# The last projection of a decoder trunk: operand sums and the residual by accumulating DMA in place of GpSimd additions

## Chip, cores and metric

The kernel runs on one NeuronCore of a Trainium2 chip. The metric is the device time of one execution in microseconds (us); the kernel before took 1645.27 us (median of three runs, 1644.04 to 1647.09). Engines are named as in the profile: PE (TensorE, the matmuls), PEld (its weight loads), DVE (VectorE), ACT (ScalarE), POOL (GpSimd), SP (SyncE, which here only issues DMAs). L686 is line 686 of the kernel.

## What is computed

A trunk of two residual layers and a final norm on x of 1024 tokens by 1024 channels, all in float32:

```python
h_res = x
h_res = h_res + even_layer(rmsnorm(h_res, norm_g[0]))    # state-space and pooling mixers
h = rmsnorm(h_res, norm_g[1])
z = h @ w_in                                             # 1024 x 8192
x_in, b_gate, c_gate, g = split(z, 4)
conv = causal_conv3(c_gate * x_in) + conv_b
y = b_gate * conv * silu(g)                              # 1024 tokens x 2048 channels
h_res = h_res + y @ w_out                                # w_out 2048 x 1024: the last projection
return rmsnorm(h_res, final_g)
```

The change concerns the last two lines: `y @ w_out`, the residual added to it, and the way into the final norm.

## The kernel before

**Precision.** Every large matmul runs on float32 values split in two parts, a rounded part h and the rest l = x - h (`split_to`, L78: ScalarE writes h, VectorE writes l, L81/L82 or with a scale L84/L85). A product is three matmuls: h weight by h activation, h by l, l by h.

**The last projection** is one product of 2 x 2 blocks by Winograd's form of Strassen's scheme: seven products of half-size operands instead of eight, each with operands that are blocks or sums of blocks. The contraction's halves are channels 0 to 1023 and 1024 to 2047 of y; the other halves are the first and second 512 tokens (`H0`, `H1`) and the even and odd 128-row blocks of the output. The seven products are numbered and run in the order `JT = (1, 5, 7, 6, 4, 2, 3)`. Each takes four weight tiles of 128 x 1024 (p = 0 to 3), so there are 28 weight tiles w = 0 to 27, product `JT[w // 4]`, tile p = w % 4.

**Steps.** A step t (`j_mm`, L1004) is the 24 matmuls of one weight tile: eight blocks n, three matmuls each. Steps 0 to 23 work on 512 columns; the last product (3) runs in two quarters of 256 columns, so steps 24 to 31 are half steps with tiles 24 to 27 twice. Results land in six halves of three PSUM tiles in turn. `j_post(t - 1)` (L1020), run at the beginning of step t, adds step t - 1's result into one to three quarters of the two output tiles `o` of row pair p (product 1 is copied by ScalarE instead).

**What each product needs.** Activations live in one tile `x` of eight blocks: x0(n) is the H0 half and x1(n) the H1 half of block n; b22 is a separate tile in the slots `td0` and `td1`. In place, block by block, `jb_sum` (L937) makes the operands of products 5, 7, 6 and 4 ("T4"), and `jb_split` splits them; products 1, 2 and 3 take plain blocks. On the weight side a tile S per p is kept in place: `jw_load` (L957) loads blocks on SP's queue, `jw_sum` (L973) makes the sums of products 5, 7, 6 and 3 on GpSimd (16 in all), `jw_split` (L983) splits into a ring of two h and two l tiles. GpSimd also does half of the block sums of products 5, 7 and 6, all eight of T4's, and the residual: `res_load` brings a 128 x 1024 block of the residual stream on SP's queue, `res_add` (L1040) adds it to `o` on GpSimd, eight times.

**What sets the order.** It is written out by hand. Every engine executes its own list in order and waits for semaphores; SP's and POOL's queues are also in order. `j_pre[t]` (from L1321) lists what is put on the engines ahead of step t's matmuls: splits one step before use, weight sums two, weight loads three. `sc_tail` (L1313) does the same for the last seven steps of the layer's input projection (`run_pairs`, L728), where loads and first splits of the last projection begin. `end2()` (L1504) returns the last two products of the layer before (`b * t`, VectorE, and a store of each to `y2d`), which are run ahead of step 0's matmuls. From step 18 on squares of finished rows are summed for the final norm, and from step 28 on VectorE and GpSimd scale the output by the norm and SP stores it.

Of the kernel before, what the change touches and what calls it, by code (L numbers as in the profile page):

```python
# [8 lines left out]
F32 = mybir.dt.float32  # L9
F32R = mybir.dt.float32r  # L10
I32 = mybir.dt.int32
AF = mybir.ActivationFunctionType
ALU = mybir.AluOpType

P = 128
T = 1024
# [11 lines left out]
def trunk(ctx: ExitStack, tc: tile.TileContext, a: dict, out: bass.AP):  # L28
# [4 lines left out]
    wp = ctx.enter_context(tc.tile_pool(name="wp", bufs=2))  # L33
# [5 lines left out]
    V, A, G, PE, S = nc.vector, nc.scalar, nc.gpsimd, nc.tensor, nc.sync  # L39
    LD = nc.scalar  # L40
    ctr = [0]

    def slot(tag, shape, dtype=F32):
        ctr[0] += 1
        return sp.tile(shape, dtype, tag=tag, name=f"{tag}_{ctr[0]}")
# [27 lines left out]
    def act_tiles(k, shape=(T,)):  # L73
        t = act_slot(k, [P, 2, *shape])
        act[k] = (t[:, 0], t[:, 1])
        return act[k]

    def split_to(h, l, src, scale=None, e=None):  # L78

        if scale is None:  # L80
            A.activation(h, src, AF.Copy)  # L81
            (e or V).tensor_tensor(out=l, in0=src, in1=h, op=ALU.subtract)  # L82
        else:
            A.activation(h, src, AF.Copy, scale=scale)  # L84
            V.scalar_tensor_tensor(out=l, in0=src, scalar=scale, in1=h, op0=ALU.mult, op1=ALU.subtract)  # L85
# [51 lines left out]
    def at(d, s, f):  # L137
        d.setdefault(s, []).append(f)
# [42 lines left out]
    y2d = dp.tile([16, P, T], F32, name="y2d")  # L181
    hrd = [dp.tile([P, T], F32, name=f"hrd{k}") for k in range(NK)]
# [45 lines left out]
    def tt(e, o, x, y, op):  # L228
        e.tensor_tensor(out=o, in0=x, in1=y, op=op)  # L229
# [169 lines left out]
    def u_load(k, tag):  # L399
        t = slot(tag, [P, 8, NC])  # L400
        LD.dma_start(t, ud[k].rearrange("(g h) j c -> (h j) g c", g=8))
        s5["U"][k] = t
# [205 lines left out]
    H0, H1 = slice(0, 512), slice(512, T)  # L608
# [298 lines left out]
    J_ = {"T": {}, "o": {}, "w": {}, "raw": {}, "h": {}, "bank": {}, "ring": 0, "acc": [None] * 3}  # L907
    JT = (1, 5, 7, 6, 4, 2, 3)
    JO = {0: (HB[0], HB[1]), 1: (HB[4], HB[5]), 2: (HB[2], HB[3]), 3: (HB[6], HB[7])}

    def y2_load(o, n0, n, hs):
        S.dma_start(o, y2d[n0 : n0 + n, :, hs].rearrange("n p t -> p n t"))

    def x_load(k, hs):

        if "x" not in J_:
            J_["x"] = slot("big", [P, 8, T])
        y2_load(J_["x"][:, 2 * k : 2 * k + 2, hs], 2 * k, 2, hs)

    def b21_load(k):  # L920
        y2_load(J_["x"][:, 2 * k : 2 * k + 2, H1], 8 + 2 * k, 2, H0)

    def y22_load(k):
        if k % 2 == 0:
            J_["y22", k // 2] = slot(f"td{k // 2}", [P, 4, 512])
        y2_load(J_["y22", k // 2][:, 2 * (k % 2) : 2 * (k % 2) + 2], 8 + 2 * k, 2, H1)

    def x0(n):
        return J_["x"][:, n, H0]

    def x1(n):
        return J_["x"][:, n, H1]

    def b22(n):
        return J_["y22", n // 4][:, n % 4]

    def jb_sum(i, n, e):  # L937
        if i == 5:
            tt(e, x0(n), x1(n), x0(n), ALU.subtract)
        elif i == 7:  # L940
            tt(e, x1(n), b22(n), x1(n), ALU.subtract)
        elif i == 6:
            tt(e, x0(n), b22(n), x0(n), ALU.subtract)
        elif i == 4:
            tt(e, x0(n), x1(n), x0(n), ALU.subtract)

    def jb_split(i, n):
        if n % 2 == 0:
            J_["B", i, n // 2] = act_tiles(4 * (JT.index(i) % 2) + n // 2, (2, 512))
        h, l = J_["B", i, n // 2]  # L950
        src = {1: x0, 5: x0, 7: x1, 6: x0, 4: x0, 2: x1, 3: b22}[i](n)
        split_to(h[:, n % 2], l[:, n % 2], src, 0.5)


    JS = ("t9", "t6", "t4", "t5")

    def jw_load(w):  # L957
        i, p = JT[w // 4], w % 4
        src = {1: (2 * p,), 5: (2 * p + 1, 9 + 2 * p), 7: (2 * p + 1,), 6: (9 + 2 * p,), 4: (9 + 2 * p,),
               2: (8 + 2 * p,), 3: (8 + 2 * p,)}[i]  # L960
        r = J_["raw", w] = []
        for j, m in enumerate(src):
            ctr[0] += 1
            if i == 1:
                t = J_["S", p] = slot(JS[p], [P, T])
            elif i == 5 and p % 2:
                t = slot(f"t{j}", [P, T])
            else:
                t = wp.tile([P, T], F32, tag="raw", name=f"raw_{ctr[0]}")
            S.dma_start(t, scout[m])  # L970
            r.append(t)

    def jw_sum(w):  # L973
        i, p = JT[w // 4], w % 4
        r = J_["raw", w]
        if i == 5:
            tt(G, r[0], r[0], r[1], ALU.add)
        elif i == 7:
            tt(G, J_["S", p], J_["S", p], r[0], ALU.subtract)
        elif i in (6, 3):  # L980
            tt(G, J_["S", p], r[0], J_["S", p], ALU.subtract)

    def jw_split(w):  # L983
        i, p = JT[w // 4], w % 4
        if i == 3 and p > 1:
            t = slot(f"td{p - 2}", [P, 2, T], F32R)
            h, l = t[:, 0], t[:, 1]
        else:
            ctr[0] += 1
            h = wp.tile([P, T], F32R, tag="whi", name=f"whi_{ctr[0]}")  # L990
            l = wp.tile([P, T], F32R, tag="wlo", name=f"wlo_{ctr[0]}")
        J_["w", w] = (h, l)
        split_to(h, l, J_["S", p] if i in (1, 7, 6, 3) else J_["raw", w][0])

    def j_slot(t):

# [36 lines left out]
            for d, x in {5: ((1, 0),), 7: ((3, 1), (2, 0)), 6: ((1, 1), (2, 2), (3, 3)), 4: ((2, 2),), 2: ((0, 0),)}[i]:  # L1033
                tt(V, q[d], q[x], bk, ALU.add)

    def res_load(m):
        J_["h", m] = slot(f"t{2 + m // 2 % 2}", [P, T])
        S.dma_start(J_["h", m], hrd[m])

    def res_add(m):  # L1040
        o = J_["o", m // 2][m % 2]
        tt(G, o, o, J_["h", m], ALU.add)

    def j_sq2(p):

        o = J_["o", p][1]
        if p == 0:
            J_["ss"] = slot("t1", [P, T])
            A.activation(J_["ss"], o, AF.Square)
        else:  # L1050
            J_["sq"] = slot("t0", [P, T])
            A.activation(J_["sq"], o, AF.Square)
            tt(V, J_["ss"], J_["ss"], J_["sq"], ALU.add)
        A.activation(o, o, AF.Copy, scale=gf[:, 2 * p + 1 : 2 * p + 2])
# [33 lines left out]
    win, wout, glu, scin, scout, pw = a["win"], a["wout"], a["glu"], a["scin"], a["scout"], a["pw"]  # L1088
# [46 lines left out]
    for k in range(8):  # L1135

        s = 6 + k // 2
        t, x = t_work(k), x_work(k - 1) if k else [lambda: None] * 2
        b = [lambda k=k: z_build(k + 2)] if k < 6 else []
        n = [lambda k=k: u_load(k + 1, UT[(k + 1) % 2])] if k < 7 else []  # L1140
        if k % 2 == 0:
            o = [lambda k=k, i=i: odd_work[k // 2 - 1][i]() for i in range(4)] if k else [lambda: None] * 4
# [160 lines left out]
    for k in range(4):  # L1303
# [7 lines left out]


    sc_tail = {-2: [lambda: jw_load(0), lambda: jw_load(1)],  # L1313
               1: [lambda: jw_load(4)],
               2: [lambda: jw_load(2), lambda: [x_load(k, H0) for k in range(4)]],
               3: [lambda: jw_load(3), lambda: [x_load(k, H1) for k in range(4)]],
               4: [lambda: [jb_split(1, n) for n in range(4)]],
               5: [lambda: jw_split(0), lambda: [jb_split(1, n) for n in range(4, 8)], lambda: jw_load(5)]}


    j_pre, j_mid = {}, {}  # L1321
    NS = 32
    for w in range(4, 28):
        at(j_pre, w - 2, lambda w=w: jw_sum(w))
    for w in range(1, 28):
        at(j_pre, w - 1, lambda w=w: jw_split(w))
    for w in range(6, 28):
        at(j_pre, w - 3, lambda w=w: jw_load(w))
    for x in range(6):
        i = JT[x + 1]  # L1330
        for n in range(8):
            if x == 0:
                at(j_pre, n // 2, lambda i=i, n=n: jb_sum(i, n, G if n % 2 else V))
            at(j_pre, 4 * x + n // 2, lambda i=i, n=n: jb_split(i, n))
    for x in range(1, 6):
        for n in range(8):
            at(j_pre, 4 * x + n // 2 - 1, lambda i=JT[x + 1], n=n: jb_sum(i, n, G if i == 4 or n % 2 else V))
    for k in range(4):
        at(j_pre, 1 + k // 2, lambda k=k: y22_load(k))
        at(j_pre, 5 + k, lambda k=k: b21_load(k))  # L1340
    for p in range(4):
        at(j_pre, 12 + p, lambda p=p: res_load(2 * p + 1))
        at(j_pre, 14 + p, lambda p=p: res_add(2 * p + 1))
        at(j_pre, 17 + p, lambda p=p: res_load(2 * p))
        at(j_pre, 19 + p, lambda p=p: res_add(2 * p))
        at(j_pre, 18 + p, lambda p=p: j_sq2(p))
        at(j_pre, 22 + p, lambda p=p: j_sq(p, H0))
    rH, rQ = j_rms(H0, False), [j_rms(at_q(q), True) for q in range(2)]
# [150 lines left out]
    late = []  # L1499
    for t in range(NS):  # L1500
        if t:
            j_post(t - 1)
        else:
            late = end2()  # L1504
        for f in j_pre.get(t, []):
            f()
        for f in late:
            f()
        late = []
        j_mm(t, j_mid.get(t, {}))  # L1510
    j_post(NS - 1)
    for f in j_pre[NS] + rQ[1]:
# [71 lines left out]
```

## Time and profile before

| what | value |
|---|---|
| median of three runs (lowest, highest) | 1645.27 us (1644.04, 1647.09) |
| the profiled execution: its own time | 1644.73 us |
| its span | 1642.9 us |
| mean granted PE clock | 0.977 |
| PE, DVE, ACT, POOL busy | 96%, 71%, 34%, 47% of the span |

The span is the time from the first to the last instruction; the execution's own time is 1.8 us longer, and lies 0.54 us under the median. Times in the trace count from the span's start. "Busy" of PE counts overlapping matmuls by their modelled ends, so a busy PE can still run slower than it could. An idle time is put down to the engine whose semaphore came last.

### The profile page before, as it was taken

How to read it: one execution, taken by the hardware profiler on the slowest of the kernel's cores; microseconds unless marked ns; L12 is line 12 of the kernel's file. 1: busy time of each engine (PE TensorE's matmuls, PEld its weight loads, DVE VectorE, ACT ScalarE, POOL GpSimd, SP SyncE). 2: the span in 40 equal slices, each digit the busy share in tenths (PEclk: the TensorE clock that was granted, in tenths of full speed). 3: DMA queues.
4: the chain of work that ended last, by engine and by line, in shares of the span. 5: the costliest groups of instructions: out<-in, count | busy, mean ns of one | idle time of the engine just before them, and what ended most of it. 6: DMA issues, size and time to landing. Idle time of an engine off the chain costs nothing.

```text
span 1642.9 us, 19135 instructions
## 1 busy us (share of the span) xinstructions
PE 1573.6 (96%) x7138; PEld 1301.5 (79%) x7138; DVE 1164.3 (71%) x1308; ACT 559.4 (34%) x840; POOL 772.2 (47%) x686
## 2 busy tenths in 40 slices
PE   9899999999999999999879999999999999997996
PEld 7688888877788788888658888888888888875776
DVE  5545655688555776652798696868677786899986
ACT  5245111123353433332433233332323232432363
POOL 6952599707322532101465353434353443458643
PEclk9999999999999999999879999999999999999997
DMA  6232632214687432233211212212121212454242
GB/s 212 94 124 90 159 110 84 77 63 137 187 285 240 145 115 78 77 116 136 95 37 67 78 52 77 78 52 102 53 77 52 77 52 92 165 204 151 81 153 104
DMA packets 94348, 181.83 MB, mean 111 GB/s; under 512 B 16432, under 2 KB 53040, under 8 KB 93744
## 3 DMA queue, kind: packets, MB, share of 16 engines
q1 hardware_dynamic: 55584, 93.05, 16.9%
q10 hardware_dynamic: 38672, 87.57, 16.3%
q8 instruction: 57, 0.93, 0.2%
q14 instruction: 35, 0.29, 0.1%
HBM read 141.85 MB, written 42.93 MB: 112 GB/s over the span
## 4 chain that ended last, share of the span: by engine, by line
PE 54%; DVE 10%; issue 1%; DMA 1%; ACT 1%; POOL 1%; DVEq 0%; ACTq 0%
PE acc L686 44%; PE acc L1018 5%; PE acc L114 4%; DVE a L85 3%; DVE wlo L82 2%; PE acc L837 1%; DVE t L229 1%; DVE big L229 1%; DVE ws L82 1%; DMA t<-in_glu 0%; DVE a L82 0%; POOL t L229 0%; DVE B L229 0%; DMA hpd<-t 0%; PE aux L168 0%
## 5 line engine op out<-in xcount | busy, mean ns | idle before, releaser
L686 PE MATMUL acc<-a,ws 128*128 128x512 f32 x1920 | 451.4, 391 | 3.9 <-DVE LR L229 1.6
L686 PEld LDWEIGHTS acc<-a,ws 128*128 128x128 f32 x1920 | 361.7, 189 | 81.5 <-ACT a L81 3.1
L114 PE MATMUL acc<-a,whi 128*128 128x512 f32 x1440 | 395.0, 396 | 2.6 <-DVE t L229 2.6
L114 PEld LDWEIGHTS acc<-a,whi 128*128 128x128 f32 x1440 | 269.8, 190 | 58.1 <-issue 4.0
L229 POOL TENSOR_TENSOR t<-t,t 128x512 f32<-128x512 f32 (+2 forms) x85 | 158.7, 1867 | 302.8 <-DVE ws L82 183.7
L81 ACT ACTIVATE ws<-t 128x512 fp32r<-128x512 f32 x200 | 125.8, 630 | 338.7 <-PE acc L686 199.8
L686 PE MATMUL acc<-big,ws 128*128 128x512 f32 x960 | 230.8, 396 | 10.8 <-DVE big L82 3.9
L686 PEld LDWEIGHTS acc<-big,ws 128*128 128x128 f32 x960 | 182.8, 191 | 52.3 <-DVE ws L82 5.5
L114 PE MATMUL acc<-a,wlo 128*128 128x512 f32 x720 | 222.8, 391 | 0.0
L82 DVE TENSOR_TENSOR ws<-t,ws 128x512 fp32r<-128x512 f32 x200 | 182.6, 913 | 32.5 <-ACT ws L81 30.7
L82 DVE TENSOR_TENSOR wlo<-raw,whi 128x1024 fp32r<-128x1024 f32 (+2 forms) x67 | 92.6, 1386 | 100.1 <-ACT whi L81 100.0
L114 PEld LDWEIGHTS acc<-a,wlo 128*128 128x128 f32 x720 | 136.0, 189 | 29.0
L1018 PE MATMUL acc<-a,whi 128*128 128x512 f32 (+1 forms) x448 | 137.3, 390 | 3.2 <-ACT whi L81 1.6
L229 DVE TENSOR_TENSOR t<-t,acc 128x512 f32<-128x512 f32 x140 | 94.9, 680 | 51.0 <-PE acc L686 50.9
L686 PE MATMUL acc<-td,ws 128*128 128x512 f32 x480 | 118.2, 395 | 0.3 <-DVE td L82 0.3
L81 ACT ACTIVATE whi<-raw 128x1024 fp32r<-128x1024 f32 (+2 forms) x67 | 63.5, 952 | 143.7 <-PE acc L114 120.8
L229 POOL TENSOR_TENSOR t<-C,LR 128x1024 f32<-128x1024 f32 (+1 forms) x18 | 41.7, 2320 | 143.2 <-PE aux L491 64.9
L686 PEld LDWEIGHTS acc<-td,ws 128*128 128x128 f32 x480 | 91.2, 190 | 21.3 <-issue 1.4
L1018 PE MATMUL acc<-a,wlo 128*128 128x512 f32 (+1 forms) x224 | 88.7, 396 | 16.6 <-DVE wlo L82 16.6
L1018 PEld LDWEIGHTS acc<-a,whi 128*128 128x128 f32 x448 | 86.6, 199 | 20.5 <-DVE a L85 2.4
L229 POOL TENSOR_TENSOR raw<-raw,raw 128x512 f32<-128x512 f32 (+1 forms) x22 | 32.0, 1455 | 128.3 <-DVE ws L82 121.0
L81 ACT ACTIVATE ws<-raw 128x512 fp32r<-128x512 f32 x80 | 50.0, 626 | 74.4 <-PE acc L686 51.7
(283 smaller groups left out, 2138.2 us busy)
## 6 DMA issues: line engine op xcount, KB each, us to landing
raw<-in_scin ACTq DMA_DIRECT2D x32, 512.0 KB, 4.0
t<-in_scin ACTq DMA_DIRECT2D x32, 512.0 KB, 4.3
raw<-in_win ACTq DMA_DIRECT2D x29, 512.0 KB, 3.6
raw<-in_scout SPq DMA_DIRECT2D x24, 512.0 KB, 4.1
t<-ud ACTq DMA_DIRECT2D x16, 512.0 KB, 4.3
raw<-in_wout ACTq DMA_DIRECT2D x16, 512.0 KB, 3.7
big<-y2d SPq DMA_DIRECT2D x12, 512.0 KB, 5.6
ud<-t SPq DMA_DIRECT2D x8, 512.0 KB, 2.9
```

The source lines that it names most:

```text
L81: A.activation(h, src, AF.Copy)
L82: (e or V).tensor_tensor(out=l, in0=src, in1=h, op=ALU.subtract)
L85: V.scalar_tensor_tensor(out=l, in0=src, scalar=scale, in1=h, op0=ALU.mult, op1=ALU.subtract)
L114: PE.matmul(acc[:, n * 512 : n * 512 + 512], lhsT=w, rhs=x[:, n * 512 : n * 512 + 512], start=first and i == 0, stop=last and i == 2)
L229: e.tensor_tensor(out=o, in0=x, in1=y, op=op)
L686: PE.matmul(bank, lhsT=wt, rhs=x[:, k], start=k == 0 and j == 0, stop=k == 3 and j == 2)
L837: PE.matmul(u.acc[:, hs], lhsT=w, rhs=x[:, hs], start=k == 0 and j == 0, stop=k == NK - 1 and j == 2)
L1018: PE.matmul(bank, lhsT=w, rhs=x[:, n % 2, c], start=n == 0 and j == 0, stop=n == 7 and j == 2)
```

## The change

All of it is in the last projection.

- Weight sums: the tile of the first block is completed in place by a DMA that adds the second block from DRAM (`accum_op=add`, issued on GpSimd's queue), without GpSimd adding. Where a difference is wanted (products 7 and 3) ScalarE first negates the tile in place. 16 accumulating transfers and 8 negations take the place of 16 loads and 16 GpSimd sums. The sign of product 7's weights turns, and that of its activations with it.
- T4: ScalarE negates x0 (two blocks at a time) and a DMA adds B21 from `y2d`: four negations, four accumulating transfers.
- Residual: `res_load` goes; `res_add` is an accumulating transfer from DRAM straight into `o`.
- All block sums of products 5, 7 and 6 run on VectorE.
- Product 3 reads B22 from `x` again (four new loads, `b22_load`), so `td0` and `td1` are free earlier and the splits of tiles 26 and 27 move to steps 18 and 20.
- Times: sums of product 5 in steps 0 and 1 (the first in the layer before), of 7 in steps 3 to 6, of 6 in 8 to 11, T4 in 9 to 12, of 3 in 13 to 16, residual in 14 to 17 and 18 to 21. Loads of B21 move from steps 5 to 8 to steps 12 to 15.
- The last two products of the layer before run in steps 1 and 2 instead of together in step 0.

The core of the diff:

```diff
         elif i == 7:
-            tt(e, x1(n), b22(n), x1(n), ALU.subtract)
+            tt(e, x1(n), x1(n), b22(n), ALU.subtract)
         elif i == 6:
             tt(e, x0(n), b22(n), x0(n), ALU.subtract)
-        elif i == 4:
-            tt(e, x0(n), x1(n), x0(n), ALU.subtract)
+    def neg(t):
+        A.activation(t, t, AF.Copy, scale=-1.0)
+    def plus(t, src):
+        G.dma_start(t, src, accum_op=ALU.add)
+    def t4_sum(k):
+        x = J_["x"][:, 2 * k : 2 * k + 2, H0]
+        neg(x)
+        plus(x, y2d[8 + 2 * k : 10 + 2 * k, :, H0].rearrange("n p t -> p n t"))
+    def b22_load(k):
+        y2_load(J_["x"][:, 2 * k : 2 * k + 2, H0], 8 + 2 * k, 2, H1)
...
     def jw_load(w):
...
+        if i == 1:
+            t = J_["S", p] = slot(JS[p], [P, T])
+        elif i == 5 and p > 1:
+            t = slot(f"t{p - 2}", [P, T])
+        else:
+            t = wp.tile([P, T], F32, tag="raw", name=f"raw_{ctr[0]}")
+        J_["raw", w] = t
+        S.dma_start(t, scout[{1: 2 * p, 5: 2 * p + 1, 4: 9 + 2 * p, 2: 8 + 2 * p}[i]])
     def jw_sum(w):
         i, p = JT[w // 4], w % 4
-        r = J_["raw", w]
-        if i == 5:
-            tt(G, r[0], r[0], r[1], ALU.add)
-        elif i == 7:
-            tt(G, J_["S", p], J_["S", p], r[0], ALU.subtract)
-        elif i in (6, 3):
-            tt(G, J_["S", p], r[0], J_["S", p], ALU.subtract)
+        t = J_["raw", w] if i == 5 else J_["S", p]
+        if i in (7, 3):
+            neg(t)
+        plus(t, scout[{5: 9 + 2 * p, 7: 2 * p + 1, 6: 9 + 2 * p, 3: 8 + 2 * p}[i]])
...
     def res_add(m):
-        o = J_["o", m // 2][m % 2]
-        tt(G, o, o, J_["h", m], ALU.add)
+        plus(J_["o", m // 2][m % 2], hrd[m])
...
     sc_tail = {-2: [lambda: jw_load(0), lambda: jw_load(1)],
+               2: [lambda: [x_load(k, H0) for k in range(4)], lambda: jw_load(4)],
+               3: [lambda: jw_load(2), lambda: [x_load(k, H1) for k in range(4)]],
+               4: [lambda: [jb_split(1, n) for n in range(4)], lambda: jw_load(5)],
+               5: [lambda: jw_split(0), lambda: [jb_split(1, n) for n in range(4, 8)], lambda: jw_load(3),
+                   lambda: jw_load(6), lambda: jw_load(7), lambda: jw_sum(4)]}
...
     for w in range(1, 28):
-        at(j_pre, w - 1, lambda w=w: jw_split(w))
+        at(j_pre, {26: 18, 27: 20}.get(w, w - 1), lambda w=w: jw_split(w))
...
+    for x in (1, 2):
         for n in range(8):
+            at(j_pre, 4 * x + n // 2 - 1, lambda i=JT[x + 1], n=n: jb_sum(i, n, V))
     for k in range(4):
+        at(j_pre, 1 + (k + 1) // 2, lambda k=k: y22_load(k))
+        at(j_pre, 9 + k, lambda k=k: t4_sum(k))
+        at(j_pre, 12 + k, lambda k=k: b21_load(k))
+        at(j_pre, 16 + k, lambda k=k: b22_load(k))
     for p in range(4):
+        if p:
+            at(j_pre, p // 2, lambda p=p: jw_sum(4 + p))
+        at(j_pre, 3 + p, lambda p=p: jw_sum(8 + p))
+        at(j_pre, 8 + p, lambda p=p: jw_sum(12 + p))
+        at(j_pre, 13 + p, lambda p=p: jw_sum(24 + p))
+        at(j_pre, 13 + p, lambda p=p: jw_load(16 + p))
+        at(j_pre, 17 + p, lambda p=p: jw_load(20 + p))
         at(j_pre, 14 + p, lambda p=p: res_add(2 * p + 1))
-        at(j_pre, 19 + p, lambda p=p: res_add(2 * p))
+        at(j_pre, 18 + p, lambda p=p: res_add(2 * p))
...
         for f in j_pre.get(t, []):
             f()
-        for f in late:
-            f()
-        late = []
+        if t in (1, 2):
+            late[t - 1]()
         j_mm(t, j_mid.get(t, {}))
```

## Rows read from the trace of the kernel before

**Rows 1.** Page, part 1: busy time, share of the span and instructions.

```profile
PE 1573.6 (96%) x7138; PEld 1301.5 (79%) x7138; DVE 1164.3 (71%) x1308; ACT 559.4 (34%) x840; POOL 772.2 (47%) x686
```

**Rows 2.** Stretches of 20 us: busy (count) by engine, PE clock, DMA share, GB/s.

```profile
1500.00:1520.00 20.00, 15.12 (x60) 11.62 (x58) 20.00 (x14) 5.26 (x7) 19.92 (x10) 0.91 0.52 175
1540.00:1560.00 20.00, 20.00 (x89) 16.32 (x88) 20.00 (x19) 8.41 (x12) 10.65 (x4) 1.00 0.30 101
```

**Rows 3.** The matmuls' line L1018: its instructions, and who ended its idle time.

```profile
L1018 PE MATMUL acc<-a,whi x448: 277/389/632, 1439.4 to 1621.7; 128*128 128x512 f32 x128, 128*128 128x256 f32 x22
...
  DVE wlo L82: 36.6, 17
```

**Rows 4.** Chain of waits, 1425 to 1643: start, us, what.

```profile
1501.93 4.50 DVE a L85 x2
1506.44 1.70 DVE big L229
...
1528.53 39.51 PE acc L1018 x165
```

**Rows 5.** Timeline of DVE: start, us, instructions, idle before them.

```profile
1470.28 4.59 DVE L85 SCALAR_TENSOR_TENSOR a<-big,a 128x512 fp32r<-128x512 f32 x2
...
1475.99 3.14 DVE L82 TENSOR_TENSOR wlo<-raw,whi 128x1024 fp32r<-128x1024 f32 x1
...
1496.44 1.28 DVE L85 SCALAR_TENSOR_TENSOR a<-big,a 128x512 fp32r<-128x512 f32 x2
1497.64 0.68 DVE L229 TENSOR_TENSOR big<-td,big 128x512 f32<-128x512 f32 x1
...
1537.24 1.22 DVE L82 TENSOR_TENSOR wlo<-t,whi 128x1024 fp32r<-128x1024 f32 x1
```

**Rows 6.** Timeline of POOL.

```profile
1470.16 2.45 POOL L229 TENSOR_TENSOR raw<-raw,raw 128x1024 f32<-128x1024 f32 x1 [7.21 <-DMA raw<-in_scout]
1472.57 1.75 POOL L229 TENSOR_TENSOR big<-td,big 128x512 f32<-128x512 f32 x1
```

**Rows 7.** Groups by shape, 1437 to 1643: busy us, mean ns, idle before.

```profile
L85 DVE SCALAR_TENSOR_TENSOR a<-big,a 128x512 fp32r<-128x512 f32 x45 | 64.3, 1468 | 2.8 <-ACT a L84 2.8
...
L1054 ACT ACTIVATE t<-t,vec 128x1024 f32<-128x1024 f32 x2 | 2.3, 1155 | 0.1
```

**Rows 8.** Timeline of ACT (ScalarE).

```profile
1546.09 1.06 ACT L81 ACTIVATE whi<-raw 128x1024 fp32r<-128x1024 f32 x1 [3.29 <-PE acc L1018]
...
1551.53 1.06 ACT L81 ACTIVATE whi<-raw 128x1024 fp32r<-128x1024 f32 x1 [3.34 <-PE acc L1018]
```

**Rows 9.** Timeline of SP's queue.

```profile
1565.58 0.33 SPq L970 DMA_DIRECT2D raw<-in_scout  x1
```

**Rows 10.** Stretches of 4 us, PE alone: busy (count), clock, DMA share, GB/s.

```profile
1436.00:1440.00 4.00, 4.00 (x19) 1.00 1.06 393
1604.00:1608.00 4.00, 4.00 (x21) 0.50 0.00 0
```

**Rows 11.** DMA issues, 1425 to 1643: count, size, median us to landing.

```profile
raw<-in_scout SPq DMA_DIRECT2D x22, 512.0 KB, 3.9
...
t<-in_scout SPq DMA_DIRECT2D x5, 512.0 KB, 7.5
```

**Rows 12.** Timeline of PE at the half steps.

```profile
1595.28 0.40 PE L1018 MATMUL acc<-a,whi 128*128 128x256 f32 x2
...
1596.08 0.40 PE L1018 MATMUL acc<-a,whi 128*128 128x256 f32 x2
...
1596.44 0.40 PE L1018 MATMUL acc<-a,whi 128*128 128x256 f32 x2
...
1600.04 0.50 PE L1018 MATMUL acc<-a,whi 128*128 128x256 f32 x2 [1.64 <-ACT whi L81]
1602.79 0.58 PE L1018 MATMUL acc<-a,wlo 128*128 128x256 f32 x1 [2.26 <-DVE wlo L82]
...
1624.70 3.58 PE L1018 MATMUL acc<-a,td 128*128 128x256 f32 x27
```

More of the change, by code (lines that the diff above doesn't have):

```diff
@@ L950, in jb_split @@
         h, l = J_["B", i, n // 2]
-        src = {1: x0, 5: x0, 7: x1, 6: x0, 4: x0, 2: x1, 3: b22}[i](n)
+        src = {1: x0, 5: x0, 7: x1, 6: x0, 4: x0, 2: x1, 3: x0}[i](n)
         split_to(h[:, n % 2], l[:, n % 2], src, 0.5)
@@ L958, in jw_load @@
         i, p = JT[w // 4], w % 4
[L959 to L971, printed above, removed]
+        ctr[0] += 1
+        if i == 1:
[6 more added lines that the diff above has]
+        S.dma_start(t, scout[{1: 2 * p, 5: 2 * p + 1, 4: 9 + 2 * p, 2: 8 + 2 * p}[i]])
     def jw_sum(w):
         i, p = JT[w // 4], w % 4
-        r = J_["raw", w]
-        if i == 5:
-            tt(G, r[0], r[0], r[1], ALU.add)
-        elif i == 7:
-            tt(G, J_["S", p], J_["S", p], r[0], ALU.subtract)
-        elif i in (6, 3):
-            tt(G, J_["S", p], r[0], J_["S", p], ALU.subtract)
+        t = J_["raw", w] if i == 5 else J_["S", p]
+        if i in (7, 3):
+            neg(t)
+        plus(t, scout[{5: 9 + 2 * p, 7: 2 * p + 1, 6: 9 + 2 * p, 3: 8 + 2 * p}[i]])
     def jw_split(w):
@@ L992, in jw_split @@
         J_["w", w] = (h, l)
-        split_to(h, l, J_["S", p] if i in (1, 7, 6, 3) else J_["raw", w][0])
+        split_to(h, l, J_["S", p] if i in (1, 7, 6, 3) else J_["raw", w])
     def j_slot(t):
@@ L1034, in j_post @@
                 tt(V, q[d], q[x], bk, ALU.add)
-    def res_load(m):
-        J_["h", m] = slot(f"t{2 + m // 2 % 2}", [P, T])
-        S.dma_start(J_["h", m], hrd[m])
     def res_add(m):
-        o = J_["o", m // 2][m % 2]
-        tt(G, o, o, J_["h", m], ALU.add)
+        plus(J_["o", m // 2][m % 2], hrd[m])
     def j_sq2(p):
@@ L1313, in trunk @@
     sc_tail = {-2: [lambda: jw_load(0), lambda: jw_load(1)],
[L1314 to L1318, printed above, removed]
+               2: [lambda: [x_load(k, H0) for k in range(4)], lambda: jw_load(4)],
[3 more added lines that the diff above has]
+                   lambda: jw_load(6), lambda: jw_load(7), lambda: jw_sum(4)]}
     j_pre, j_mid = {}, {}
     NS = 32
-    for w in range(4, 28):
-        at(j_pre, w - 2, lambda w=w: jw_sum(w))
     for w in range(1, 28):
-        at(j_pre, w - 1, lambda w=w: jw_split(w))
-    for w in range(6, 28):
-        at(j_pre, w - 3, lambda w=w: jw_load(w))
+        at(j_pre, {26: 18, 27: 20}.get(w, w - 1), lambda w=w: jw_split(w))
     for x in range(6):
@@ L1332, in trunk @@
             if x == 0:
-                at(j_pre, n // 2, lambda i=i, n=n: jb_sum(i, n, G if n % 2 else V))
+                at(j_pre, n // 2, lambda i=i, n=n: jb_sum(i, n, V))
             at(j_pre, 4 * x + n // 2, lambda i=i, n=n: jb_split(i, n))
-    for x in range(1, 6):
+    for x in (1, 2):
         for n in range(8):
-            at(j_pre, 4 * x + n // 2 - 1, lambda i=JT[x + 1], n=n: jb_sum(i, n, G if i == 4 or n % 2 else V))
+            at(j_pre, 4 * x + n // 2 - 1, lambda i=JT[x + 1], n=n: jb_sum(i, n, V))
     for k in range(4):
-        at(j_pre, 1 + k // 2, lambda k=k: y22_load(k))
-        at(j_pre, 5 + k, lambda k=k: b21_load(k))
+        at(j_pre, 1 + (k + 1) // 2, lambda k=k: y22_load(k))
+        at(j_pre, 9 + k, lambda k=k: t4_sum(k))
+        at(j_pre, 12 + k, lambda k=k: b21_load(k))
+        at(j_pre, 16 + k, lambda k=k: b22_load(k))
     for p in range(4):
-        at(j_pre, 12 + p, lambda p=p: res_load(2 * p + 1))
+        if p:
[5 more added lines that the diff above has]
+        at(j_pre, 17 + p, lambda p=p: jw_load(20 + p))
         at(j_pre, 14 + p, lambda p=p: res_add(2 * p + 1))
-        at(j_pre, 17 + p, lambda p=p: res_load(2 * p))
-        at(j_pre, 19 + p, lambda p=p: res_add(2 * p))
+        at(j_pre, 18 + p, lambda p=p: res_add(2 * p))
         at(j_pre, 18 + p, lambda p=p: j_sq2(p))
```

## The prediction

> **What bounds the kernel now.** I read the page first: PE is busy 96% of the span [rows 1], so time can only come out of stretches where PE waits or runs slowly. The stretches of 20 us place the change: in 1500 to 1520 PE is busy 15.12 us at a mean clock of 0.91, while DVE is busy all 20.00 us and POOL 19.92; in 1540 to 1560 PE is busy throughout at full clock [rows 2]. So in the first part of the last projection (it starts at 1439.4) DVE has no time left, and PE's longest waits on its line are for DVE's weight split: 36.6 us in 17 waits (matmuls and weight loads counted each) [rows 3]. The chain of waits says the same: around 1500 it is made of DVE work alone, and only from 1528.53 does it run on PE [rows 4].
>
> Why DVE is full is in its timeline. A pair of activation splits (L85) takes 1.28 us at 1496.44 but 4.59 us at 1470.28; a weight split takes 1.22 us at 1537.24 but 3.14 us at 1475.99; a 512-column sum takes 0.68 us [rows 5]. The long ones lie beside POOL's sums: POOL worked from 1470.16 to about 1474.3, 2.45 and 1.75 us [rows 6], and the 4.59 us end at 1474.87. DVE loses about as much as POOL works. Over the stage the mean of an L85 split is 1.468 us instead of 0.64, 45 times [rows 7]: 37 us lost in that line alone.
>
> Where PE is not held up, a step's weight split on ScalarE starts every 5.44 us (1546.09, 1551.53, both released by PE) [rows 8]. That is the pace of a step of 24 matmuls with 512 columns.
>
> **The change, part by part.**
>
> *POOL's sums go.* All 44 of the stage's POOL sums before the norms vanish: 16 weight sums, 20 block sums, 8 residual sums. What DVE loses beside POOL goes with them. This is the gain.
>
> *DVE takes 12 block sums more* (half of those for products 5, 7 and 6): 12 x 0.68 = 8.2 us. Does DVE fit into a step of 5.44 us? The fullest are steps 9 and 10: two results added (1.3, taken like the 0.68), a weight split 1.22, two block sums 1.36, a split pair 1.28: 5.2 us [rows 5]. Steps 1 and 2 have one weight split, two sums, a split pair, a moved product of the layer before (the two that stood together in step 0; I take 1.2, as for the weight split of that size) and a ScalarE wait of well under 1 us between sum and split: also close to 5.4. Steps 12 to 23 are under 4.6, as T4 leaves DVE and POOL alike. So DVE stays just below PE if nothing holds it. Nothing covers an excess there: it would come out on PE.
>
> *ScalarE negates* 8 weight blocks and 4 pairs of activation blocks: 12 x 1.155 us [rows 7], at most two in a step, beside two splits and a weight half of about 1 us each [rows 8]. Under 5 us in any step, after the weight split in its queue; cost nothing while PE's step covers them. T4's negation waits for DVE's split of the step before; the next weight split is queued behind it, but that one has to wait for PE's step to end anyway.
>
> *The queues.* SP issues 24 loads fewer (16 weight blocks, 8 residuals) and 4 more (B22 read again); each costs it 0.33 us [rows 9], and SP is never what ends. POOL issues 28 accumulating transfers in their place, one of them in the last steps of the layer before, 27 in steps 0 to 21. What an issue costs POOL is not in this trace: at least SP's 0.33 us, at most about the 2.45 us of the sum it replaces [rows 6, 9]. At two per step, either end fits into 5.44 us; nothing else waits in POOL's queue until the norms. I take 1 us, nearer to an issue than to an addition.
>
> *The price of one accumulating transfer* (512 KB) decides. The trace has none. Below: a plain load at 393 GB/s in 1436 to 1440 [rows 10], 0.524 MB/393 GB/s = 1.33 us of all DMA engines. Above: 7.5 us, the slowest median from issue to landing of such a load here, as if each waited for the one ahead [rows 11]. I take 2 x 1.33 = 2.7 us, since the old contents must be read as well as the new, nearest the plain load. The Trainium skill states a rule that speaks against the change (Collectives: The Full Stack, section "The bandwidth ceiling: the fold count and why AG ≠ RS ≠ AR"): a transfer that adds is half as fast as a copy because it reads two sources. No row here shows it; by it the price would also be 2.7 us.
>
> What must it fit? The densest stretch is steps 8 to 17: 16 accumulates (4 each for the weights of products 6 and 3, T4, odd residuals) and 11 plain loads. Time there: 10 x 5.44 = 54.4 us. Need: 16 x 2.7 + 11 x 1.33 = 57.8 us. The excess of 3.4 us is covered: each accumulate is issued three steps (16.3 us) or more before DVE or ScalarE needs it, against 2 or 3 us of use and some 4 us to landing as for a plain load [rows 11]. So nothing is late at my price.
>
> *Sum.* Before, the 24 full steps ran from 1439.4 to 1595.28, where the first 256-column matmul starts [rows 3, 12]: 155.9 us. At PE's pace they take 24 x 5.44 = 130.6: 25.3 us less. In the eight half steps after that, three matmuls take 0.36 us, but PE waited 1.64 us for ScalarE and 2.26 us for DVE (both behind POOL's last weight sums), and then ran four microseconds at a clock of 0.50 (1.2 of 2.4 GHz) [rows 10, 12], costing 2.0. Two of the four last weight splits move to steps 18 and 20, and the sums come early: 5.9 us less. Together 31.2 us. The end after PE's last projection matmul (1628.28) [rows 12] is untouched, norms on POOL included. The profiled execution took 1644.73 us, so 1613.5; the median of the runs shown is 0.54 above it: **1614 us**. The forecast's own range: 1608 (a little of the other waits goes too) to 1622 (two steps' worth of stalls stay).
>
> **Rivals.**
>
> *A. The transfers become the bound (slower).* In steps 8 to 17 no gain is lost while 16P + 14.7 stays under 54.4 + 16.3 = 70.7, P = 3.5 us. The whole gain is lost at 16P = 70.7 + 31.2 - 14.7, P = 5.4 us. From there the kernel is slower. At 7.5 us one after another, with the plain loads alongside, 120 - 70.7 = 49 us are lost against 31 won: 1644.7 + 18 = 1663 us, with DVE and ScalarE waiting for the sums, and PE for them. For it: landing times of 7.5 us do occur when transfers queue [rows 11]. Against: that row lies in the burst of loads; the other weight loads take 3.9. Chance 0.18.
>
> *B. Issuing on POOL holds DVE as adding did (faster, but less).* If an issue took 1.5 us and cost DVE as much, steps 8 to 11 would need 4.8 (5.2 less the overlap of consecutive DVE instructions, which start about 0.07 before the last one's end [rows 5]) + 3.0 = 7.8 us: 2.4 x 4 = 9.4 lost; steps 13 to 17 about 6.6: 1.2 x 5 = 6. In all some 16 us: 1630 us. A price P of 4.5 for the transfers would come out at the same time. For: DVE's budget is thin. Against: an issue moves no data through POOL. Chance 0.20.
>
> *C. The gain is given back in full* (P between 5 and 5.6, or A in part): 1645 us. Chance 0.07.
>
> **How the numbers follow.** Forecast 0.55, A 0.18, B 0.20, C 0.07. A measurement can tell 0.2% (3.3 us) of this kernel from no change. Faster is the forecast with B: 0.75; same is C: 0.07; slower is A: 0.18. The range goes from the forecast's low end to C: 1608 to 1645, holding forecast, B and most of C, about 0.8; A is left out.
>
> **What would show it.** Right: L85 pairs at 1.3 us and weight splits at 1.2 throughout the stage, POOL empty of sums, ScalarE's weight halves 5.44 us apart from the first steps on, PE clock at 1.00 up to the norms, no wait of PE on the weight split beyond a microsecond. A: ScalarE or DVE waiting for a transfer in the last projection, DMA engines busy without a break in steps 8 to 17. B: L85 splits still long, with POOL issuing beside them. The prediction is wrong if landing of an accumulate takes over 10 us, or if DVE is still back to back while PE waits.

## The result and the profile after

The changed kernel took 1621.3 us (median of four runs, 1618.9 to 1625.5) beside 1644.8 for the kernel before: a ratio of 0.9858, interval 0.9835 to 0.9880, so some 23 us less. The forecast was 1614, with a range of its own to 1622. The profiled execution has a span of 1623.7 us and took 1625.5, the slowest of the four; its step 0 begins at 1442.1, where that of before began at 1439.4 [rows 3]. Those 2.7 us arose far ahead of the change (the last matmul of line L114, in the layer before, starts at 777.3 instead of 774.6) and have to be added to the difference of the spans (19.2) to get what the last projection won: 21.9 us.

The page, parts 1 and 3 (part 3: packets, MB, share of 16 engines' span); the first row answers to [rows 1], q0 is the new queue, GpSimd's:

```profile
PE 1560.7 (96%) x7138; PEld 1291.7 (80%) x7138; DVE 1111.7 (68%) x1320; ACT 570.9 (35%) x852; POOL 692.9 (43%) x670
...
q0 software_dynamic: 4544, 14.68, 4.8%
```

Groups by shape from 1439 on, answering to [rows 7]; the second is what an issue of an accumulating transfer costs POOL:

```profile
L85 DVE SCALAR_TENSOR_TENSOR a<-big,a 128x512 fp32r<-128x512 f32 x54 | 35.0, 684 | 5.6 <-ACT a L84 5.6
...
L950 POOL DMA_DIRECT2D t<-in_scout x14 | 13.8, 983 | 44.2 <-ACT t L946 38.3 <-DVE wlo L82 5.5 <-issue 0.4
```

The timeline of DVE (start, us, instructions), answering to [rows 5]:

```profile
1494.56 1.22 DVE L82 TENSOR_TENSOR wlo<-t,whi 128x1024 fp32r<-128x1024 f32 x1
...
1501.14 1.28 DVE L85 SCALAR_TENSOR_TENSOR a<-big,a 128x512 fp32r<-128x512 f32 x2
```

The mean L85 split takes 0.684 us instead of 1.468, a pair 1.28 and a weight split 1.22 wherever one looks. POOL adds nothing until the norms. Its timeline has issues in place of the additions of [rows 6]:

```profile
1501.93 1.20 POOL L950 DMA_DIRECT2D big<-y2d  x1 [3.23 <-ACT big L946]
...
1535.09 1.21 POOL L950 DMA_DIRECT2D t<-hrd  x1
1535.63 1.56 POOL L950 DMA_DIRECT2D LR<-hrd  x1
...
1537.24 2.61 POOL L950 DMA_DIRECT2D K<-hrd  x1
```

The pair at 1501.14 runs beside the issue at 1501.93 and still takes 1.28 us: this issue does not hold DVE. From 1535.09 on five residuals are issued: one odd, then the four even ones (1535.63 to 1537.24, the middle two left out here), which the text of the kernel places in steps 18 to 21, in one go around the start of step 17 (tile 18's split, at 1536.65 below). They start some 0.54 us apart and their rows overlap, so 1.56 to 2.61 us are not the price of one issue. Nothing on POOL's queue made them wait.

PE's line of matmuls and what ended its idle time (us, times), answering to [rows 3], where the last line was 36.6, 17:

```profile
L1025 PE MATMUL acc<-a,whi x448: 277/389/628, 1442.1 to 1602.6; 128*128 128x512 f32 x128, 128*128 128x256 f32 x22
...
L1025 PE MATMUL acc<-a,td x96: 278/283/681, 1588.7 to 1608.9; 128*128 128x256 f32 x96
...
  ACT whi L81: 11.6, 6
  DVE wlo L82: 5.4, 8
```

The chain of waits (start, us, what), answering to [rows 4]:

```profile
1471.71 59.70 PE acc L1025 x262
...
1534.49 9.79 DMA raw<-in_scout
...
1546.73 16.63 DMA raw<-in_scout
```

From 1471.71 on it runs on PE, where it ran on DVE before; then it has two long pieces of a weight load. ScalarE's weight splits, one for each step, show where the pace of 5.44 us [rows 8] is missed (idle time before them and what ended it in brackets):

```profile
1449.94 1.05 ACT L81 ACTIVATE whi<-t 128x1024 fp32r<-128x1024 f32 x1
...
1455.89 1.05 ACT L81 ACTIVATE whi<-t 128x1024 fp32r<-128x1024 f32 x1
...
1462.15 1.05 ACT L81 ACTIVATE whi<-raw 128x1024 fp32r<-128x1024 f32 x1
...
1469.35 1.05 ACT L81 ACTIVATE whi<-raw 128x1024 fp32r<-128x1024 f32 x1
...
1487.74 1.06 ACT L81 ACTIVATE whi<-t 128x1024 fp32r<-128x1024 f32 x1 [3.34 <-issue]
...
1536.65 1.06 ACT L81 ACTIVATE whi<-raw 128x1024 fp32r<-128x1024 f32 x1 [2.39 <-PE acc L1025]
...
1544.38 1.06 ACT L81 ACTIVATE whi<-raw 128x1024 fp32r<-128x1024 f32 x1 [5.63 <-DMA raw<-in_scout]
...
1554.28 1.06 ACT L81 ACTIVATE whi<-raw 128x1024 fp32r<-128x1024 f32 x1 [4.71 <-DMA raw<-in_scout]
...
1563.46 1.06 ACT L81 ACTIVATE whi<-raw 128x1024 fp32r<-128x1024 f32 x1 [4.95 <-DMA raw<-in_scout]
...
1582.97 1.06 ACT L81 ACTIVATE whi<-t 128x1024 fp32r<-128x1024 f32 x1 [2.06 <-PE acc L1025]
```

Two stretches are slow. The splits of tiles 2 to 5 (the first four rows) are 5.95, 6.26 and 7.20 us apart; from step 0 (1442.1) to the split at the start of step 8 (tile 9, 1487.74) 2.1 us are lost. And the splits of tiles 19, 20 and 21 wait 5.63, 4.71 and 4.95 us for their loads: from tile 18's split (1536.65, step 17) to tile 25's (1582.97, step 24) 46.3 us pass where 7 x 5.44 = 38.1 would do: 8.2 us lost. Without both, 21.9 + 10.3 = 32.2 us would have been won, against the 31.2 of the forecast's sum. The time from issue to landing of such loads, and of the last even residual, from 1500 to 1600:

```profile
raw<-in_scout SPq DMA_DIRECT2D x6, 512.0 KB, 9.5
...
K<-hrd POOLq DMA_DIRECT2D x1, 512.0 KB, 26.3
```

The load issued at 1546.73 (the last row of the chain above) is there for ScalarE at 1563.46: over 16 us for 512 KB that took 3.9 us before [rows 11]. The DMA engines were about full from 1500 on; from 1535 to 1560 their mean busy share is 1.05 to 1.06 (stretches, columns as in [rows 2]):

```profile
1500.00:1505.44 5.44, 5.44 (x26) 4.50 (x25) 4.83 (x8) 3.05 (x5) 2.14 (x2) 1.00 1.09 197
...
1517.88:1523.32 5.44, 5.44 (x26) 4.50 (x25) 4.22 (x7) 3.05 (x5) 1.80 (x2) 1.00 0.86 145
...
1565.00:1570.00 5.00, 4.65 (x15) 3.40 (x14) 5.00 (x7) 4.97 (x7) 0.00 (x0) 0.66 0.37 111
```

The last row shows that part of the 8.2 us is not waiting itself: behind the waits for tiles 20 and 21 PE's mean granted clock was 0.66.

The cause of the late loads could be in the engines (accumulating transfers fill them), or in the issue (with two raw tiles, each load waits for the split of the tile two before).

### The profile page after: what moved, and what is told of

Read it like the earlier page. It is cut to its first block, busy times and chain, and to the rows that moved or that the text cites. A ratio compares the mean times of both kernels' runs of the same rounds, so it can differ in the third digit from the quotient of the medians.

```text
span 1623.7 us, 19133 instructions
## 1 busy us (share of the span) xinstructions
PE 1560.7 (96%) x7138; PEld 1291.7 (80%) x7138; DVE 1111.7 (68%) x1320; ACT 570.9 (35%) x852; POOL 692.9 (43%) x670
## 4 chain that ended last, share of the span: by engine, by line
PE 80%; DVE 9%; DMA 4%; POOL 2%; ACT 2%; issue 2%; SPq 1%; ACTq 0%; DVEq 0%; POOLq 0%
PE acc L686 44%; PE acc L114 25%; PE acc L1025 6%; DVE t L229 2%; DMA raw<-in_scout 2%; DVE wlo L82 1%; PE acc L837 1%; PE aux L393 1%; DVE big L229 1%; PE aux L410 1%; POOL td L229 1%; DVE a L82 1%; DVE ws L82 1%; POOL td L233 1%; DVE a L85 1%
## 5 line engine op out<-in xcount | busy, mean ns | idle before, releaser
L114 PE MATMUL acc<-a,whi 128*128 128x512 f32 x1440 | 394.2, 396 | 4.2 <-DVE t L229 2.6
L114 PEld LDWEIGHTS acc<-a,whi 128*128 128x128 f32 x1440 | 269.1, 189 | 59.9 <-issue 4.0
L229 POOL TENSOR_TENSOR t<-t,t 128x512 f32<-128x512 f32 (+2 forms) x81 | 146.8, 1813 | 295.4 <-DVE ws L82 183.7
L114 PE MATMUL acc<-a,wlo 128*128 128x512 f32 x720 | 222.7, 391 | 0.0
L114 PEld LDWEIGHTS acc<-a,wlo 128*128 128x128 f32 x720 | 135.9, 189 | 28.9
L1025 PE MATMUL acc<-a,whi 128*128 128x512 f32 (+1 forms) x448 | 131.2, 377 | 5.2 <-ACT whi L81 5.2
L686 PEld LDWEIGHTS acc<-td,ws 128*128 128x128 f32 x480 | 90.7, 189 | 21.9 <-DVE td L82 1.7
L1025 PEld LDWEIGHTS acc<-a,whi 128*128 128x128 f32 x448 | 82.4, 190 | 21.3 <-ACT whi L81 6.5
L1025 PE MATMUL acc<-a,wlo 128*128 128x512 f32 (+1 forms) x224 | 84.8, 378 | 1.7 <-DVE wlo L82 1.7
L229 POOL TENSOR_TENSOR raw<-raw,raw 128x512 f32<-128x512 f32 x20 | 26.7, 1336 | 121.1 <-DVE ws L82 121.0
```

The source lines that it names most:

```text
L114: PE.matmul(acc[:, n * 512 : n * 512 + 512], lhsT=w, rhs=x[:, n * 512 : n * 512 + 512], start=first and i == 0, stop=last and i == 2)
L686: PE.matmul(bank, lhsT=wt, rhs=x[:, k], start=k == 0 and j == 0, stop=k == 3 and j == 2)
L1025: PE.matmul(bank, lhsT=w, rhs=x[:, n % 2, c], start=n == 0 and j == 0, stop=n == 7 and j == 2)
```

## Experiments

Each was compared with the kernel before on the same chip; x1 to x4 in one session, x5 to x8 in another, x9 in a third. The changed kernel stands at 0.9858 of the kernel before; across sessions it is better to compare ratios than times, since the kernel before had medians of 1644.8 to 1647.6 us in them. "Lost" below is read from ScalarE's weight splits as above.

**x1: plain copies.** Nothing but the addition in the transfer goes, so the tiles get the second block instead of the sum.

```diff
-        G.dma_start(t, src, accum_op=ALU.add)
+        G.dma_start(t, src)
```

> The 28 accumulating transfers become plain transfers from the same queue, at the same places (the tile gets the second block instead of the sum; the additions are left out). Theory 1 (the DMA engines are full because an accumulating transfer costs twice a plain one, about 2.8 us against 1.4 us of all engines, so the weight loads of products 4 and 2 land late): the engines have room again, loads land in about 4 us, steps 18 to 23 run at 5.44 us, about 8 us less than the changed kernel: near 1613 us. Theory 2 (the loads are late because each waits for one of the two raw tiles and so is issued too late, whatever the engines do): landing and time stay, near 1621 us.

1614.0 us, ratio 0.9800 (0.9785 to 0.9814). All weight splits from step 16 on are 5.44 us apart. The page, part 3, and the loads' time to landing from 1500 to 1600:

```profile
q0 software_dynamic: 4032, 14.68, 2.6%
```

```profile
raw<-in_scout SPq DMA_DIRECT2D x6, 512.0 KB, 4.0
```

The share of the queue gives the price. Accumulating: 4.8% of 1623.7 us over 28 transfers is 2.78 us of all engines each; plain: 2.6% of 1611.9 us is 1.50 us. With more room in the engines the same loads, issued by the same rule, land in 4.0 us. That is theory 1; under theory 2 nothing would have changed.

**x2: no residual.** The eight residual transfers are left out, and so is the addition of the residual.

```diff
     def res_add(m):
-        plus(J_["o", m // 2][m % 2], hrd[m])
+        return
```

> The eight residual transfers are left out (the residual is not added). Theory 1 (the burst of residual transfers, the last four of them issued four steps ahead of their place, stands in the DMA engines before the weight loads): steps 18 to 23 run at 5.44 us, near 1613 us. Theory 2 (two raw tiles, issue too late): no change, near 1621 us. Between the two (1616 to 1618): the residual has only a part in it, and the other accumulating transfers the rest.

1614.2 us, 0.9798 (0.9782 to 0.9815): all that the late loads had cost. The loads land in 3.9 us:

```profile
raw<-in_scout SPq DMA_DIRECT2D x6, 512.0 KB, 3.9
```

So beside 20 accumulating transfers the loads land as fast as before; it takes the residual's eight on top to make them late.

**x3: four tiles.** The transfers stay; the loads of tiles 18, 19, 22 and 23 get slots of their own and need not wait for a raw tile.

```diff
         elif i == 5 and p > 1:
             t = slot(f"t{p - 2}", [P, T])
+        elif i in (4, 2) and p > 1:
+            t = slot(f"t{p}", [P, T])
```

> The weights of products 4 and 2 use four tiles (two raw, two free slots) instead of two, so their loads are issued two steps or more earlier; nothing else changes, the DMA engines carry the same bytes. Theory 1 and theory 2 both expect the loads of tiles 18 to 23 in time and the 8 us back, near 1613 us, theory 1 with landing times still over 8 us, theory 2 with landing near 4 us. If the engines cannot carry the load of the stage at all (need above supply over the whole stage), the wait only moves to a later load and the time stays near 1621 us.

1615.3 us, 0.9802 (0.9787 to 0.9816), no split waits for a load, and yet the loads from 1500 to 1600 land as late as ever:

```profile
t<-in_scout SPq DMA_DIRECT2D x3, 512.0 KB, 17.1
...
raw<-in_scout SPq DMA_DIRECT2D x2, 512.0 KB, 10.1
```

So the engines stay full, as theory 1 said, but the loads are issued early enough. With x1 and x2 this shows that the loss needs both: full engines, and loads with little more than a step of lead.

**x4: order of the sums.** In steps 0 to 3 both block sums of product 5 precede the splits, those of the next pair follow them.

```diff
-            if x == 0:
-                at(j_pre, n // 2, lambda i=i, n=n: jb_sum(i, n, V))
+            if x == 0 and n < 2:
+                at(j_pre, -1, lambda i=i, n=n: jb_sum(i, n, V))
             at(j_pre, 4 * x + n // 2, lambda i=i, n=n: jb_split(i, n))
-    for x in (1, 2):
-        for n in range(8):
+    j_pre[0] = j_pre.pop(-1) + j_pre[0]
+    for x in (0, 1, 2):
+        for n in range(0 if x else 2, 8):
```

> In steps 0 to 3 the block sums of product 5 are issued ahead of the splits that wait for ScalarE, not between them; nothing else changes. If the 2.3 us that the changed kernel loses in steps 0 to 4 come from VectorE waiting 0.70 us twice in each step for ScalarE, the weight splits of tiles 2 to 6 stand 5.44 us apart and about 2 us are won: near 1619 us, seen in the trace rather than in the time. If the moved products of the layer before set the pace instead, the splits in steps 2 and 3 stay over 6 us apart and nothing is won.

1619.9 us, 0.9836 (0.9821 to 0.9851); the interval overlaps that of the changed kernel, so the time alone does not tell. The splits do. In the changed kernel DVE waited for ScalarE after every sum (the 0.70 in brackets):

```profile
1446.21 0.68 DVE L229 TENSOR_TENSOR big<-big 128x512 f32<-128x512 f32 x1
1447.60 0.69 DVE L85 SCALAR_TENSOR_TENSOR a<-big,a 128x512 fp32r<-128x512 f32 x1 [0.70 <-ACT a L84]
...
1449.59 0.69 DVE L85 SCALAR_TENSOR_TENSOR a<-big,a 128x512 fp32r<-128x512 f32 x1 [0.70 <-ACT a L84]
```

In x4 the splits of tiles 2 to 4 are 5.44 us apart, and those of tiles 19 to 21 wait for their loads as in the changed kernel (tile 19's is the last row; 4.72 and 4.89 us for the others):

```profile
1441.95 1.05 ACT L81 ACTIVATE whi<-t 128x1024 fp32r<-128x1024 f32 x1
...
1447.39 1.05 ACT L81 ACTIVATE whi<-t 128x1024 fp32r<-128x1024 f32 x1
...
1452.83 1.05 ACT L81 ACTIVATE whi<-raw 128x1024 fp32r<-128x1024 f32 x1
...
1535.85 1.06 ACT L81 ACTIVATE whi<-raw 128x1024 fp32r<-128x1024 f32 x1 [5.48 <-DMA raw<-in_scout]
```

**x5: x3 and x4 together.**

> Both earlier edits together: four weight tiles for products 4 and 2, and the sums of product 5 ahead of the splits in steps 0 to 3. If the two losses are separate, their gains add: all weight splits 5.44 us apart from step 0 on, and 8 + 2 us less than the changed kernel, near 1612 us. If the earlier steps only bring the DMA backlog nearer, the gain is that of the four tiles alone, near 1615 us.

1612.3 us (1611.8 to 1613.6), 0.9788 (0.9774 to 0.9803): the fastest version here, and its interval lies clear of the changed kernel's. The two losses were separate. In its own session it is 34.5 us faster than the kernel before, where the forecast's sum was 31.2. From its first matmul of the projection (1438.9) to tile 25's split, where step 24 begins (1569.44), 130.5 us pass: the 24 x 5.44 of the forecast. Its chain of waits runs on PE without a break from the end of the layer before to the norms:

```profile
1439.07 137.75 PE acc L1027 x636
```

**x6: additions on POOL that nobody needs.** Everything stays; POOL also adds a tile to itself.

```diff
+    pad = {}
+
+    def pad_new():
+        pad["t"] = slot("t2", [P, T])
+        G.memset(pad["t"], 0.0)
+    at(j_pre, 0, pad_new)
+    for s in range(1, 18):
+        for _ in range(2):
+            at(j_pre, s, lambda: tt(G, pad["t"], pad["t"], pad["t"], ALU.add))
```

> GpSimd adds a tile of 128 x 1024 to itself twice in each of steps 1 to 17, on a tile nobody else uses; 34 additions of about 2.4 us, and nothing waits for their results. Theory A (VectorE loses as much time as GpSimd adds, so that the kernel before was bound by it): the splits beside them are long again (L85 pairs 3.5 us and more), VectorE is full, PE waits, and 15 to 25 us come back: 1635 to 1645 us. Theory B (the gain came from the earlier sums and the shorter chains between engines): the splits and the time stay, near 1621 us.

1663.2 us, 1.0096 (1.0081 to 1.0111): some 40 us slower than the changed kernel, and about 1% slower than the kernel before. I had the direction, not the size. POOL's rows, and two pairs of DVE that ran beside them, L85 splits and additions of a matmul's result (`acc`):

```profile
1522.32 6.05 POOL L229 TENSOR_TENSOR t<-t 128x1024 f32<-128x1024 f32 x2
...
1529.66 5.04 POOL L229 TENSOR_TENSOR t<-t 128x1024 f32<-128x1024 f32 x2
...
1539.09 5.05 POOL L229 TENSOR_TENSOR t<-t 128x1024 f32<-128x1024 f32 x2
```

```profile
1526.55 6.40 DVE L85 SCALAR_TENSOR_TENSOR a<-big,a 128x512 fp32r<-128x512 f32 x2
...
1542.31 1.27 DVE L229 TENSOR_TENSOR t<-K,acc 128x512 f32<-128x512 f32 x2
```

A pair of 1.28 us takes 6.40 us next to additions whose results nobody reads, so it is POOL's additions themselves that stretch DVE's work. The pair is 5.12 us too long, and POOL's additions overlap it by 1.82 (to 1528.37) and 3.29 us (from 1529.66): 5.11. In other pairs the excess is a little less than the overlap (at 1538.10, not shown, 3.00 us for 3.29). Not all of DVE's work is stretched: the pair at 1542.31, which adds a matmul's result from PSUM, takes its usual 1.27 us although POOL adds from 1539.09 to 1544.14. The stretched ones, splits and block sums, have both operands in SBUF tiles. It is not quite alone: transfers queue on POOL behind the additions, and three weight loads still wait, so not all of the 40 us is DVE's.

**x7: even residuals at their own steps.** A one-column copy on POOL from the low half of tiles 18 to 21 holds each transfer back.

```diff
+    pace = cp.tile([P, 1], F32, name="pace")
...
-        at(j_pre, 18 + p, lambda p=p: res_add(2 * p))
+        at(j_pre, 18 + p, lambda p=p: (G.tensor_copy(pace, J_["w", 18 + p][1][:, 0:1].bitcast(F32)), res_add(2 * p)))
```

> The four even residual transfers wait, by a one-column copy on GpSimd, for the weight split of tiles 18 to 21, so each is issued at its own step and not four steps ahead. If the burst of these four is what makes the weight loads late, most of the 8 us come back: 1613 to 1616 us. If the engines' load up to step 17 alone is enough to make them late, the time stays near 1621 us; a late residual would then show as VectorE waiting for a transfer after step 20.

1618.4 us, 0.9829 (0.9812 to 0.9847): between the two expectations, and the interval overlaps that of the changed kernel, so the time alone does not tell. In its trace from tile 18's split to tile 25's:

```profile
1533.73 1.06 ACT L81 ACTIVATE whi<-raw 128x1024 fp32r<-128x1024 f32 x1 [2.49 <-DMA raw<-in_scout]
...
1543.66 1.06 ACT L81 ACTIVATE whi<-raw 128x1024 fp32r<-128x1024 f32 x1 [7.83 <-DMA raw<-in_scout]
...
1574.25 1.06 ACT L81 ACTIVATE whi<-t 128x1024 fp32r<-128x1024 f32 x1 [2.05 <-PE acc L1025]
```

40.5 us for seven steps: 2.4 lost instead of 8.2. By this trace the burst is the larger part of the late loads; what the engines had to carry up to step 17 still makes tile 19 wait 7.83 us.

**x8: the kernel before without POOL's sums.** Weight sums, POOL's half of the block sums, T4's and the residual's additions are left out.

```diff
     def jw_sum(w):
+        return
...
     def jb_sum(i, n, e):
+        if e is G:
+            return
...
     def res_add(m):
+        return
```

> The kernel before, with GpSimd's sums of the last projection left out (weight sums, its half of the block sums, T4, residual); nothing is moved to VectorE, ScalarE or DMA. Theory A (GpSimd's work beside VectorE is the whole loss): every step at 5.44 us, 31 us less than before, near 1614 to 1616 us. Theory B (the places of loads and sums bound it as well): it stays over 1625 us, with PE waiting for loads.

1614.2 us, 0.9797 (0.9782 to 0.9811). With loads, splits and steps where they were, the pace is PE's, also in the stretch that was DVE's before (from the first matmul at 1439.3 to tile 25's split at 1569.84 it is again 130.5 us):

```profile
1493.74 1.06 ACT L81 ACTIVATE whi<-t 128x1024 fp32r<-128x1024 f32 x1 [3.34 <-PE acc L1021]
...
1499.18 1.06 ACT L81 ACTIVATE whi<-t 128x1024 fp32r<-128x1024 f32 x1 [3.34 <-PE acc L1021]
```

Leaving the sums out also takes away the waits for their results, so x8 alone would not separate the two; with x6, where no operation waits for the added sums and DVE's work is stretched all the same, it does.

**x9: the residual alone.** The kernel before with `res_load` gone and the accumulating transfer in `res_add`.

```diff
     def res_load(m):
+        return
...
-        tt(G, o, o, J_["h", m], ALU.add)
+        G.dma_start(o, hrd[m], accum_op=ALU.add)
```

> The kernel before with one part of the change alone: the eight residual sums leave GpSimd and become accumulating transfers in the same steps, the eight residual loads on SP go. If what counts is GpSimd's work beside VectorE where VectorE sets the pace, little is won, since from step 13 on PE set the pace already although GpSimd added there: 1642 to 1646 us. If GpSimd's additions cost time wherever they lie, a quarter of their busy time was the residual's, and some 6 to 8 us are won: near 1638 us.

1643.1 us (ten runs), 0.9981 (0.9970 to 0.9991): 3 us won, the first expectation. The stretches of 20 us (columns as in [rows 2]):

```profile
1500.00:1520.00 20.00, 16.28 (x59) 12.66 (x57) 20.00 (x14) 5.37 (x7) 19.98 (x9) 0.83 0.40 132
1540.00:1560.00 20.00, 20.00 (x90) 16.53 (x90) 15.35 (x22) 7.80 (x12) 5.23 (x6) 1.00 0.72 151
```

DVE is as full as ever from 1500 to 1520; from 1540 to 1560 POOL is down from 10.65 to 5.23 us and PE, busy throughout before and after, gains nothing. From the split of tile 14 to that of tile 24:

```profile
1533.95 1.06 ACT L81 ACTIVATE whi<-t 128x1024 fp32r<-128x1024 f32 x1 [5.68 <-PE acc L1018]
...
1588.36 1.06 ACT L81 ACTIVATE whi<-t 128x1024 fp32r<-128x1024 f32 x1 [2.12 <-PE acc L1018]
```

54.4 us, which is 10 x 5.44. The kernel before took 56.8 for the same splits (1535.27 to 1592.02), and there the last one waited 4.26 us for its weight sum, which had itself waited for its load. So the 3 us come from the last weight splits and not from DVE's full stretch. Whether the residual's sums on POOL or its loads on SP's queue had made them late is not shown, as x9 takes away both.

## Why the prediction was right, and where its sum was short

**What bounded the kernel: right.** DVE beside POOL's additions. Taking the additions out (x8) brings 5.44 us a step; putting others in (x6) brings the stretched splits back, by about as much as POOL adds beside them. That a part outside DVE's stretch wins little is x9.

**The full steps: 15.0 us won, 25.3 forecast.** From 1442.1 to tile 25's split at 1582.97 they took 140.9 us instead of 155.9; the forecast had 130.6. The 10.3 us are the two losses, 2.1 and 8.2. The time still fell into the forecast's own range, just under its end of 1622, which allowed for "two steps' worth of stalls" (10.9 us) without saying where they would come from: that the size fitted is luck.

**DVE's budget: right for steps 9 and 10, wrong for the first steps.** In the stretch from 1500.00 to 1505.44 DVE is busy 4.83 of 5.44 us (5.2 in the forecast, which added the durations without their overlap), and steps 8 to 11 held the pace. For steps 1 and 2 I counted a ScalarE wait of well under 1 us, once; it came twice in a step, 0.70 us each, as sum and split alternate block by block. That lost 2.1 us up to step 8, and x4 gives it back.

**ScalarE and the issues: right.** A negation took 1.05 us and no step waited for one from step 6 on. An issue costs POOL 0.86 to 1.2 us (I took 1), and the DVE pairs beside issues keep their 1.28 us, so rival B did not come.

**The price of a transfer: right.** 2.7 us taken, 2.78 us measured, 1.86 times the plain one from the same queue. For the adding step of a ring collective the Trainium skill (Collectives: The Full Stack, section "The bandwidth ceiling: the fold count and why AG ≠ RS ≠ AR") states that a second source read halves the rate; the forecast carried this over to a single transfer that adds. The transfers here, from DRAM into SBUF, agree with it by the 1.86 of x1; that the second read is the reason, no run here shows.

**What it must fit: here the step failed.** The sum of 57.8 us in 54.4 came out near: in the stretches of one step between 1500 and 1529 the DMA engines' mean busy share is 0.86 to 1.09. Its members were others, though, for both queues ran ahead of the text: SP had issued the loads of B21 and of tiles 16 and 17 by 1485.85, before step 8, and POOL the even residuals in step 17. I then asked only whether the accumulating transfers have enough lead, "three steps (16.3 us) or more", with "some 4 us to landing" for them, and gave the lead of the plain loads beside them no thought. Two things were missed. The loads of tiles 18 to 21 have little more than one step of lead, because each waits for a raw tile, and in full engines the late ones needed 9.8 us and more. And POOL's queue follows its waits, not the steps in the text: the four even residuals ran one to four steps ahead, into full engines. So rival A's mechanism came, in steps 18 to 20 and at a price at which I had found nothing lost; it cost 8.2 us instead of the whole gain.

**The signs.** L85 pairs of 1.28 us, weight splits of 1.22 and no sums on POOL came as forecast; the even pace from the first steps on and the clock of 1.00 up to the norms did not. The prediction named as a sign of being wrong that an accumulating transfer takes over 10 us to land. The last residual took 26.3 us. By that sign the part on the transfers was wrong, even if no wait from step 6 on is put down to an accumulating transfer, only to the loads behind them.

**The half steps: about right.** From the first 256-column matmul to the end of the projection 33.0 us were taken before [rows 12]. After, from tile 25's split at 1582.97, when step 24 begins, to the last matmul, which starts at 1608.9, it is 26 us: 7 won, 5.9 forecast. The waits for the last weight splits are gone, and with them the stretch at the lower clock at this place.

## What to carry to other kernels

Before moving work off an engine, ask what it does to its neighbour: here GpSimd's additions cost VectorE's splits and block sums about as much time as they lay beside them, and removing them was worth more than moving them cost. When transfers fill the DMA engines, check the lead of every load that shares them, not only that of the new ones, and give the loads tiles enough to be issued early. A queue runs as far ahead as its waits allow: a transfer placed late in the text is late only if something holds it there.

## What the runs showed of the hardware that I had not expected

Useless additions on POOL cost more than I expected: 34 of them, at 2.25 to 3 us, came with some 40 us, though the transfers held up behind them have a share in that. They stretch DVE's splits and block sums by about the time that they overlap (5.12 us for 5.11 in the pair of x6), but not its additions of a matmul's result from PSUM (1.27 us). Issuing a transfer on POOL keeps it busy for 0.86 to 1.2 us, and a pair of two-operand DVE instructions beside it still takes 1.28 us. An accumulating transfer of 512 KB takes 2.78 us of all DMA engines, a plain one from the same queue 1.50. And when the engines are full, the loads of the other queue are not spared: plain loads of 512 KB took 9.5 us in the median to land beside the accumulating transfers, 4.0 us when these were plain, and 3.9 us when only the residual's were left out.
